# A two-block transformer on one core: memory projections moved behind layer a, rotations by norm-scaled tables on VectorE, layer b's staging and rotation buffers parted

## The chip, the cores and the metric

The kernel runs on one core of a Trainium2 chip. A time is the device time of one execution in microseconds (us), and the number that counts is the median over the runs shown: 2902.65 us for the kernel before (three runs, 2900.12 to 2906.84). All data are float32; matrix products are done in three passes on a 32-bit matmul type (fp32r).

## The reference, cut to what matters

Two transformer blocks run in a row on 512 tokens of width 2048. The first one puts 16 meta tokens ahead (528 columns), then layer a (differential attention) and layer b (windowed attention with sinks); the second one mixes three token mixers and ends in a cross attention to 256 memory tokens.

```python
# layer a
h = rms_norm(x, norm_g)
q, k, v, gate = jnp.split(h @ w_in, 4, axis=-1)        # 8 heads; q, k in two halves of 128 rows
q = partial_rope(q, cos, sin); k = partial_rope(k, cos, sin)   # 32 of the 128 rows are rotated
o = diff_attention(q, k, v, lam, cid)
x = x + (rms_norm(o, subln_g) * (1 - lambda_init) * jax.nn.silu(gate)) @ w_out
# shared k, v of layer b, then layer b
k, v = jnp.split(rms_norm(x, kv_norm) @ w_kv, 2, axis=-1); k = partial_rope(k, cos, sin)
q, gate = jnp.split(rms_norm(x, norm_g) @ w_in, 2, axis=-1); q = partial_rope(q, cos, sin)
x = x + (swa_sink_attention(q, k, v, sinks) * jax.nn.silu(gate)) @ w_out
# second block, at its end: the memory's k and v need nothing but mem
k, v = jnp.split(rmsnorm(mem, norm_mem) @ w_kv_2, 2, axis=-1)
```

## The kernel before, in words

Activations are kept transposed: a tile has 128 features on its partitions and 528 tokens (two halves of 264) along its rows. A product `a @ w` in full accuracy is made of three matmuls: both operands are split into a high part (ScalarE copies to fp32r: `wh` of a weight, `OPH` of an activation) and a low part (VectorE subtracts: `wl`, `OPL`), and `mm3` adds high x high, low x high and high x low in PSUM. `K.proj` (L396) does one tile of 128 output features over 16 blocks of 128 inputs; `ev` then takes the sum out of PSUM (tile `pj`, three buffers). Weights come from HBM on SyncE's queue in chunks in the order of `plan` (L59); `w_next` (L381) keeps the split three pieces ahead of the matmuls.

The norm of a layer's input is a factor per token, so it is applied after the product: `norm_events` (L532) forms the factor from the sums of squares and spreads it over 128 partitions into `rbc`.

Attention is background work: a queue of generators, `K.bg`, of which `K.tick` (called once for each `mm3`) makes a step whenever `K.rate` has added up to one; `K.at` starts something at a given tick. The framework's scheduler then orders each engine's instructions by a timing of its own, so the program's order is not quite that of the code.

Four stages matter here. *Startup* (L568): the first three gate tiles of layer a (`FIRST`) are computed while x is still being loaded, block by block: each of 16 blocks needs x split, its squares added up (`add_sq`, ScalarE squares, GpSimd adds: L529) and one weight piece split. In the same stretch `mem_prep` (L596) splits the memory and adds up its squares, and the memory's k and v are projected right behind. *Layer a* (L674): per head the gate, v, q and k tiles; `rope` (L708) rotates 32 rows of each q and k tile with one shuffle on VectorE and three operations on GpSimd (tables `trig`). *out_a* (L890): the output projection, x added, sums of squares. *Layer b* (L918): k and v, then four units of q tiles and of gate tiles (`q0`, `g0`, ...); `rope` (L936) is the same on 128 rows. `windows` (L967) reads k and v back from HBM in window order. In layer b the tiles `sh` (of `rope`), `ext` (what is written to HBM), `ke` and `vx` (what is read back) share one buffer, tag `"sh"`.

Of the kernel before, what the change touches and what calls it, by code (L numbers as in the profile page):

```python
# [20 lines left out]
P = 128  # L21
# [37 lines left out]
def plan():  # L59
# [18 lines left out]
    for m in range(4):  # L78
        fm("xkv", r(128) + 128 * m)
    tm("xkv", r(512) + 512, 2)  # L80
# [183 lines left out]
class Core:  # L264
# [87 lines left out]
    def w_dma(self, i):  # L352
        while self.wi_dma <= min(i, len(self.chunks) - 1):
            off, kc, n = self.chunks[self.wi_dma]
            t = self.rp.tile([P, 1056], F32, tag="wraw", name="wraw", bufs=3)
            self.nc.sync.dma_start(
                t[:, 0:kc * n], self.a["w"][off:off + P * kc * n].rearrange("(p e) -> p e", p=P))
            self.raw[self.wi_dma] = t
            self.wi_dma += 1
# [208 lines left out]
def startup(K, dbg):  # L568
    nc, tc, a = K.nc, K.tc, K.a
    with ExitStack() as c:  # L570
        sp = c.enter_context(tc.tile_pool(name="sp", bufs=1))
        psp = c.enter_context(tc.tile_pool(name="ps_s", bufs=2, space=PSUM))
        memH = sp.tile([P, KT, NMEM], R, name="memH")
        memL = sp.tile([P, KT, NMEM], R, name="memL")
        msq = sp.tile([P, NMEM], F32, name="msq")
        rm = sp.tile([P, 5], F32, name="rm")
        rmb = sp.tile([P, NMEM], F32, name="rmb")
        xr, mr = {}, {}

        def load_x(k):  # L580
            if k < KT:
                xr[k] = sp.tile([P, T], F32, tag="xr", name="xr", bufs=4)
# [8 lines left out]
        def load_mem(i):  # L591
            if i < 4:
                mr[i] = sp.tile([P, 4, NMEM], F32, tag="mr", name="mr", bufs=2)
                nc.sync.dma_start(mr[i], a["mem"][:, 4 * i:4 * i + 4, :])

        def mem_prep():  # L596
            load_mem(0)
            load_mem(1)
            for k in range(KT):
                t = mr[k // 4][:, k % 4]  # L600
                K.split(memH[:, k], memL[:, k], t, scale=K.vcol("norm_mem_2", k))
                if k == 0:
                    nc.vector.tensor_tensor(msq, t, t, ALU.mult)
                else:
                    sq = sp.tile([P, NMEM], F32, tag="msqk", name="msqk", bufs=2)
                    nc.vector.tensor_tensor(sq, t, t, ALU.mult)
                    nc.gpsimd.tensor_tensor(msq, msq, sq, ALU.add)
                if k % 4 == 3:
                    load_mem(k // 4 + 2)
                yield  # L610


        load_x(0)
        nc.sync.dma_start(K.vec, a["vec"])
# [3 lines left out]
        K.w_dma(1)  # L618
        make_identity(nc, K.ident)
# [5 lines left out]
        K.rate = 18 / 42  # L625
        K.bg.append(mem_prep())
# [22 lines left out]

        def first_gates():  # L650
            for (h, s), f in zip(FIRST, fs):
                nc.vector.tensor_tensor(f, f, K.rbc, ALU.mult)
                th = sp.tile([P, T], F32, tag="th", name="th")
                K.act(th, f, AF.Tanh, scale=0.5)
                nc.vector.scalar_tensor_tensor(K.H[:, 2 * h + s], th, 1.0, f, ALU.add, ALU.mult)
                yield
        K.at(t0 + 12, lambda: K.bg.append(first_gates()))
        norm_events(K, sp, psp, "n", 1e-6, 0, NMEM, (t0 + 8, t0 + 15), rm, rmb, acc=msq)
        for m in range(4):
            def ev(ps, c0, c1):  # L660
                o = sp.tile([P, NMEM], F32, tag="xo", name="xo", bufs=2)
                nc.vector.tensor_tensor(o, ps, rmb, ALU.mult)
                nc.sync.dma_start(K.xkvd[:, m * NMEM:(m + 1) * NMEM], o)
            K.proj(ev, ((0, NMEM),), memH, memL)

        def evv(ps, ti, ci):
            o = sp.tile([P, 512], F32, tag="xov", name="xov", bufs=2)
            nc.scalar.activation(o, ps, AF.Copy, scale=rm[:, ti:ti + 1])
            nc.sync.dma_start(K.xkvd[:, 1024 + ti * 512:1024 + (ti + 1) * 512], o)
        K.proj_tm(evv, ((0, P), (P, 2 * P)), 512, [K.psj], memH, memL)  # L670
        K.drain()


def layer_a(K, dbg):  # L674
    nc, tc, a = K.nc, K.tc, K.a
    with ExitStack() as c:
# [20 lines left out]
        K.at(t0 + 4, lam)  # L697
# [10 lines left out]
        def rope(f):  # L708
# [140 lines left out]
        for h, base in ORDER_A:  # L849
# [5 lines left out]
            for s in range(2):  # L855
# [3 lines left out]
                K.proj(ev_scaled(f), HALVES)  # L859
# [30 lines left out]
def out_a(K, dbg):  # L890
    nc, tc, a = K.nc, K.tc, K.a
    with ExitStack() as c:
        op = c.enter_context(tc.tile_pool(name="oap", bufs=1))
        for k in range(KT):
            K.split(K.OPH[:, k], K.OPL[:, k], K.H[:, k])
        xr = {}
# [6 lines left out]
        load(1)  # L903
        for m in range(KT):
            load(m + 2)
            x = xr.pop(m)

# [4 lines left out]
            K.add_sq(op, K.H[:, m], m == 0)  # L912

# [4 lines left out]
def layer_b(K, dbg):  # L918
    nc, tc, a = K.nc, K.tc, K.a
    with ExitStack() as c:  # L920
# [30 lines left out]

        for m in range(4):
            f = bp.tile([P, T], F32, tag="f", name="f", bufs=2)
            K.proj(ev_scaled(f), HALVES)
            if m < 2:
                rope(f, 0, T)
            e = bp.tile([P, TX], F32, tag="sh", name="ext")
# [5 lines left out]
        kv = {}  # L963
        done = set()
# [982 lines left out]
```

## Time and profile before

| | |
|---|---|
| median of three runs | 2902.65 us (2900.12 to 2906.84) |
| the profiled execution | 2901.79 us, span 2900.1 us |
| TensorE (PE) busy | 2833.7 us, 98% of the span |
| VectorE (DVE), ScalarE (ACT), GpSimd (POOL) busy | 1711.9, 1302.0, 641.3 us |
| mean granted TensorE clock | 0.989 |

The span runs from the first to the last instruction; 1.7 us of the execution lie around it. Matmuls are pipelined: a matmul's own duration is over twice the distance to the next one, so the pace is read from how many start in a stretch. Idle time is given with what ended it, and only where the profile sees the engine wait.

### The profile page before, as it was taken

How to read it: one execution, taken by the hardware profiler on the slowest of the kernel's cores; microseconds unless marked ns; L12 is line 12 of the kernel's file. 1: busy time of each engine (PE TensorE's matmuls, PEld its weight loads, DVE VectorE, ACT ScalarE, POOL GpSimd, SP SyncE). 2: the span in 40 equal slices, each digit the busy share in tenths (PEclk: the TensorE clock that was granted, in tenths of full speed). 3: DMA queues.
4: the chain of work that ended last, by engine and by line, in shares of the span. 5: the costliest groups of instructions: out<-in, count | busy, mean ns of one | idle time of the engine just before them, and what ended most of it. 6: DMA issues, size and time to landing. Idle time of an engine off the chain costs nothing. (4 is left out here: it accounts for less than half of the span.)

```text
span 2900.1 us, 45499 instructions
## 1 busy us (share of the span) xinstructions
PE 2833.7 (98%) x17664; PEld 2534.4 (87%) x17664; DVE 1711.9 (59%) x3307; ACT 1302.0 (45%) x2892; POOL 641.3 (22%) x572
## 2 busy tenths in 40 slices
PE   7999999999999999989999999999999999999997
PEld 7999999999999999878877888888888877788887
DVE  8445555555566435576767733565556488774375
ACT  5333333333335323454656633455555356552253
POOL 5022022022221011123211012122332135131103
PEclk9999999999999999999999999999999999999999
DMA  5422222222222443322222243322222223224332
GB/s 184 156 87 75 74 81 81 73 81 80 74 74 66 137 137 117 123 66 73 70 78 69 73 166 130 106 81 88 77 83 89 88 81 113 82 92 128 105 113 70
DMA packets 92936, 277.05 MB, mean 96 GB/s; under 512 B 10112, under 2 KB 18192, under 8 KB 92720
## 3 DMA queue, kind: packets, MB, share of 16 engines
q1 hardware_dynamic: 91904, 273.37, 29.2%
q8 instruction: 138, 2.26, 0.3%
q10 hardware_dynamic: 816, 0.79, 0.1%
q14 instruction: 78, 0.64, 0.1%
HBM read 257.11 MB, written 17.01 MB: 95 GB/s over the span
## 5 line engine op out<-in xcount | busy, mean ns | idle before, releaser
L258 PE MATMUL pj<-OPH,wh 128*128 128x264 f32 (+1 forms) x4416 | 1459.3, 332 | 7.5 <-ACT wh L375 6.3
L258 PE MATMUL pj<-OPH,wl 128*128 128x264 f32 (+1 forms) x4416 | 1449.0, 329 | 4.2 <-DVE wl L376 4.1
L258 PE MATMUL pj<-OPL,wh 128*128 128x264 f32 (+1 forms) x4416 | 1441.2, 329 | 11.6 <-DVE OPL L472 11.6
L376 DVE TENSOR_TENSOR wl<-wraw,wh 128x512 fp32r<-128x512 f32 (+2 forms) x868 | 665.4, 769 | 638.0 <-ACT wh L375 633.0
L375 ACT ACTIVATE wh<-wraw 128x512 fp32r<-128x512 f32 (+2 forms) x868 | 544.2, 628 | 1013.8 <-PE pj L258 914.6
L258 PEld LDWEIGHTS pj<-OPH,wh 128*128 128x128 f32 x4416 | 833.1, 189 | 87.3 <-ACT wh L375 6.3
L258 PEld LDWEIGHTS pj<-OPL,wh 128*128 128x128 f32 x4416 | 830.5, 189 | 87.8 <-DVE OPL L472 13.1
L258 PEld LDWEIGHTS pj<-OPH,wl 128*128 128x128 f32 x4416 | 834.3, 189 | 74.0 <-DVE wl L376 5.2
L529 POOL TENSOR_TENSOR sumsq<-sumsq,sq 128x512 f32<-128x512 f32 (+2 forms) x101 | 122.4, 1218 | 547.9 <-ACT sq L528 511.9
L711 POOL TENSOR_TENSOR sh<-sh,trig 32x528 f32<-32x528 f32 x32 | 52.2, 1630 | 649.6 <-DVE sh L710 464.3
L258 PE MATMUL pj<-wh,OPH 128*128 128x260 f32 (+1 forms) x384 | 124.6, 325 | 0.0
L258 PE MATMUL pj<-wh,OPL 128*128 128x260 f32 (+1 forms) x384 | 123.6, 322 | 0.0
L258 PE MATMUL pj<-wl,OPH 128*128 128x260 f32 (+1 forms) x384 | 120.8, 321 | 0.0
L939 POOL TENSOR_TENSOR sh<-sh,trigb 128x512 f32<-128x512 f32 (+1 forms) x18 | 27.3, 1517 | 273.3 <-DVE sh L938 155.4
L306 ACT ACTIVATE p<-S,nmx 128x264 f32<-128x264 f32 (+5 forms) x112 | 49.7, 447 | 74.1 <-DVE nmx L758 36.8
L258 PEld LDWEIGHTS pj<-wh,OPH 128*128 128x128 f32 x384 | 72.6, 189 | 6.9 <-issue 1.5
L306 ACT ACTIVATE st<-st 128x512 f32<-128x512 f32 (+3 forms) x136 | 72.5, 550 | 12.8 <-DVE st L1164 11.1
L705 DVE TENSOR_TENSOR f<-pj,rbc 128x264 f32<-128x264 f32 x122 | 52.4, 430 | 43.4 <-PE pj L258 39.5
L258 PEld LDWEIGHTS pj<-wl,OPH 128*128 128x128 f32 x384 | 72.3, 189 | 6.2
L258 PEld LDWEIGHTS pj<-wh,OPL 128*128 128x128 f32 x384 | 72.9, 190 | 5.1
L468 ACT ACTIVATE ph<-T 80x256 fp32r<-80x256 f32 (+3 forms) x128 | 49.4, 391 | 36.4 <-DVE pl L469 18.1
L469 DVE TENSOR_TENSOR pl<-T,ph 80x256 fp32r<-80x256 f32 (+3 forms) x128 | 54.5, 432 | 14.9 <-ACT ph L468 13.9
(428 smaller groups left out, 3581.6 us busy)
## 6 DMA issues: line engine op xcount, KB each, us to landing
wraw<-in_w SPq DMA_DIRECT2D x410, 512.0 KB, 3.5
xr<-in_x SPq DMA_DIRECT2D x32, 264.0 KB, 3.5
wraw<-in_w SPq DMA_DIRECT2D x16, 520.0 KB, 3.4
xr<-hd SPq DMA_DIRECT2D x32, 256.0 KB, 2.8
hd<-H SPq DMA_DIRECT2D x16, 264.0 KB, 2.1
hd<-H SPq DMA_DIRECT2D x16, 256.0 KB, 2.0
wraw<-in_w SPq DMA_DIRECT2D x16, 256.0 KB, 2.7
wraw<-in_w SPq DMA_DIRECT2D x8, 384.0 KB, 4.7
```

The lines of the kernel that those rows point to most:

```text
L258: return self._put(self.nc.tensor.matmul(*args, **kw))
L306: i = self.nc.scalar.activation(out, in_, func, **kw)
L375: nc.scalar.activation(h[:, 0:kc * n], raw, AF.Copy)
L376: nc.vector.tensor_tensor(l[:, 0:kc * n], raw, h[:, 0:kc * n].bitcast(F32), ALU.subtract)
L468: nc.scalar.activation(hi, src, AF.Copy)
L469: eng.tensor_tensor(lo, src, hi.bitcast(F32), ALU.subtract)
L529: (eng or nc.gpsimd).tensor_tensor(acc[:, c0:c1], acc[:, c0:c1], sq[:, c0:c1], ALU.add)
L705: nc.vector.tensor_tensor(dst[:, c0:c1], ps, K.rbc[:, c0:c1], ALU.mult)
L711: nc.gpsimd.tensor_tensor(sh, sh, trig[:, 1], ALU.mult)
L939: nc.gpsimd.tensor_tensor(sh[:, c0:c1], sh[:, c0:c1], trig[:, 1, c0:c1], ALU.mult)
```

## The change

Memory: `plan` puts the `xkv` weights behind `a_out`; splits, sums and projections of the memory move from startup into `out_a`, the splits as background work (rate 17/300 a tick, from the fourth output tile), the projections behind its last tile. Startup keeps only the three gate tiles: their sums go raw to `H`, and norm, tanh and gating follow in layer a as background steps; `add_sq` of x adds on VectorE; `vec` is loaded on ScalarE's queue; the first weight chunk comes in two DMAs, x has six buffers in place of four.

Rotation: the tables are multiplied by `rbc` once (`rotation`), and `ev_rotated` multiplies the PSUM sum by the table and shuffles straight from PSUM; product and sum of the shuffled part are VectorE's, as is the low part of k in layer a. GpSimd has no part in it any more.

Layer b: `ext`, `ke` and `vx` take the two buffers of tag `"p"` (the attention's probabilities); `sh` is the rotation's alone. `windows` yields four times, not once, ahead of its transposes; the rate is 1/5 until the first attention, and .52 in place of .46 for the last unit.

```diff
@@ plan, w_dma
-    for m in range(4):
-        fm("xkv", r(128) + 128 * m)
-    tm("xkv", r(512) + 512, 2)
...
     for m in range(16):
         fm("a_out", r(128) + 128 * m)
+    for m in range(4):
+        fm("xkv", r(128) + 128 * m)
+    tm("xkv", r(512) + 512, 2)
...
+            cuts = (0, kc * n) if self.wi_dma else (0, kc * n // 2, kc * n)
@@ startup
         def x_prep(k):
-            load_x(k + 3)
+            load_x(k + 4)
...
-            K.add_sq(sp, t, k == 0)
+            K.add_sq(sp, t, k == 0, eng=nc.vector)
...
-        K.bg.append(mem_prep())
...
+                    nc.scalar.activation(K.H[:, 2 * h + s, c0:c1], psf[2 * t + i][:, 0:c1 - c0], AF.Copy)
@@ layer_a
+        def rotation():
+            nc.vector.tensor_tensor(trs, trs, K.rbc[0:32], ALU.mult)
+            nc.vector.tensor_tensor(rot[0:32], rot[0:32], K.rbc[0:32], ALU.mult)
+            for r in range(32, P, 32):
+                nc.scalar.activation(rot[r:r + 32], K.rbc[r:r + 32], AF.Copy)
...
-            nc.vector.stream_shuffle(sh, f[0:32], swap)
-            nc.gpsimd.tensor_tensor(sh, sh, trig[:, 1], ALU.mult)
-            nc.gpsimd.tensor_tensor(f[0:32], f[0:32], trig[:, 0], ALU.mult)
-            nc.gpsimd.tensor_tensor(f[0:32], f[0:32], sh, ALU.add)
+            def ev(ps, c0, c1):
+                nc.vector.tensor_tensor(dst[:, c0:c1], ps, rot[:, c0:c1], ALU.mult)
+                nc.vector.stream_shuffle(sh[:, c0:c1], ps[0:32], swap)
+                if c1 == T:
+                    nc.vector.tensor_tensor(sh, sh, trs, ALU.mult)
+                    nc.vector.tensor_tensor(dst[0:32], dst[0:32], sh, ALU.add)
...
-                    K.split(hi, lo, f, scale=None if w else SC_A, eng=nc.gpsimd if w else nc.vector)
+                    K.split(hi, lo, f, scale=None if w else SC_A)
@@ out_a
+        K.rate = 17 / 300
...
+            if m == 3:
+                K.bg.append(mem_prep())
@@ layer_b
+            def ev(ps, c0, c1):
+                nc.vector.tensor_tensor(dst[:, c0:c1], ps, trig[:, 0, c0:c1], ALU.mult)
+                nc.vector.stream_shuffle(sh[:, c0:c1], ps, swap)
+                nc.vector.tensor_tensor(sh[:, c0:c1], sh[:, c0:c1], trig[:, 1, c0:c1], ALU.mult)
+                nc.vector.tensor_tensor(dst[:, c0:c1], dst[:, c0:c1], sh[:, c0:c1], ALU.add)
...
-            e = bp.tile([P, TX], F32, tag="sh", name="ext")
+            e = bp.tile([P, TX], F32, tag="p", name="ext", bufs=2)
...
-                ke = bp.tile([P, TX], F32, tag="sh", name="ke")
+                ke = bp.tile([P, TX], F32, tag="p", name="ke", bufs=2)
...
-            vx = bp.tile([P, TX], F32, tag="sh", name="vx")
+            vx = bp.tile([P, TX], F32, tag="p", name="vx", bufs=2)
...
-            yield
+            for _ in range(4):
+                yield
...
-                K.rate = .46
+                K.rate = .46 if u < 3 else .52
```

Where instructions stand now, at two places. VectorE in startup, before, from the first memory work on (`msq`, `msqk` and `memL` are the memory's, `OPL` and `wl` the low parts of x and of the weights):

```order
L603 TENSOR_TENSOR msq<-mr 128x256
L606 TENSOR_TENSOR msqk<-mr 128x256 x2
L472 SCALAR_TENSOR_TENSOR memL<-mr,vec,memH 128x256 x4
L606 TENSOR_TENSOR msqk<-mr 128x256
L376 TENSOR_TENSOR wl<-wraw,wh 128x384
L606 TENSOR_TENSOR msqk<-mr 128x256
L472 SCALAR_TENSOR_TENSOR OPL<-xr,vec,OPH 128x528
L472 SCALAR_TENSOR_TENSOR memL<-mr,vec,memH 128x256 x4
```

The same engine and stretch now:

```order
L474 SCALAR_TENSOR_TENSOR OPL<-xr,vec,OPH 128x528
L378 TENSOR_TENSOR wl<-wraw,wh 128x384
L531 TENSOR_TENSOR sumsq<-sumsq,sq 128x528
L474 SCALAR_TENSOR_TENSOR OPL<-xr,vec,OPH 128x528
L378 TENSOR_TENSOR wl<-wraw,wh 128x384
L531 TENSOR_TENSOR sumsq<-sumsq,sq 128x528
```

The memory's operations are gone from between the two low parts, and the sum of squares, GpSimd's before, stands in their place.

VectorE in layer b before, from the first shuffle of unit q0 to its second query split (`vw` is made from the transposed `vx`, `qp` is the query split; the three products between shuffle and `qp` are GpSimd's and not in this row):

```order
L938 STREAM_SHUFFLE sh<-f 128x512
L469 TENSOR_TENSOR vw<-T,vw 128x2x64 x2
L469 TENSOR_TENSOR vw<-T,vw 80x2x64 x2
L376 TENSOR_TENSOR wl<-wraw,wh 128x512
L938 STREAM_SHUFFLE sh<-f 128x512
L376 TENSOR_TENSOR wl<-wraw,wh 128x512
L469 TENSOR_TENSOR qp<-f,qp 64x8x64 x2
L945 TENSOR_TENSOR f<-pj,rbc 128x512
```

And now, from the same tile on:

```order
L958 TENSOR_TENSOR f<-pj,trigb 128x512
L959 STREAM_SHUFFLE sh<-pj 128x512
L378 TENSOR_TENSOR wl<-wraw,wh 128x512
L960 TENSOR_TENSOR sh<-sh,trigb 128x512
L961 TENSOR_TENSOR f<-f,sh 128x512
L378 TENSOR_TENSOR wl<-wraw,wh 128x512
L471 TENSOR_TENSOR qp<-f,qp 64x8x64 x2
```

Before, the sums of the first two q tiles and most of the `vw` stand ahead of the first shuffle; now it follows its own tile's sum, ahead of the first `vw`, and the whole rotation is in VectorE's row. On TensorE the first score matmul of layer b (`S<-kxh,qp`) stands 48 projection matmuls behind the last of unit q0 before, and 36 now.

## Rows read from the trace of the kernel before

**Rows 1.** The page: busy time, share of the span, instructions.
```profile
PE 2833.7 (98%) x17664; PEld 2534.4 (87%) x17664; DVE 1711.9 (59%) x3307; ACT 1302.0 (45%) x2892; POOL 641.3 (22%) x572
```
**Rows 2.** Busy time of each engine by stage, all engines.
```profile
core 0: us, PE busy (x) PEld busy (x) DVE busy (x) ACT busy (x) POOL busy (x), PEclk, DMA share, GB/s
0.00:61.00 61.00, 42.91 (x288) 41.14 (x289) 54.88 (x70) 37.61 (x71) 39.56 (x36) 0.94 0.56 185
61.00:109.00 48.00, 48.00 (x318) 43.67 (x317) 32.06 (x72) 23.17 (x39) 0.00 (x0) 1.00 0.59 188
109.00:965.00 856.00, 855.29 (x6921) 838.36 (x6919) 474.66 (x1125) 311.30 (x761) 167.37 (x115) 1.00 0.24 79
965.00:1145.00 180.00, 179.80 (x1476) 179.77 (x1477) 68.91 (x116) 58.27 (x95) 19.92 (x15) 1.00 0.42 138
...
1215.00:1260.00 45.00, 36.98 (x164) 29.86 (x163) 30.09 (x52) 16.50 (x43) 19.30 (x12) 0.89 0.21 71
1260.00:1650.00 390.00, 380.01 (x1971) 316.00 (x1970) 276.70 (x606) 233.21 (x684) 72.08 (x48) 0.99 0.22 72
```
**Rows 3.** TensorE's timeline at the start: start, length, then idle time before.
```profile
6.33 1.69 PE L258 MATMUL pj<-OPH,wh 128*128 128x264 f32 x6 [6.33 <-ACT wh L375]
...
12.47 0.28 PE L258 MATMUL pj<-OPH,wl 128*128 128x264 f32 x1
```
**Rows 4.** What TensorE waited for, 0 to 62 us: total, times, longest.
```profile
PE pj L258 <- DVE OPL L472: 11.6, 6, 3.3
```
**Rows 5.** VectorE by line and form, 0 to 60 us: busy, mean ns.
```profile
L472 DVE SCALAR_TENSOR_TENSOR OPL<-xr,vec,OPH 128x528 fp32r<-128x528 f32 x16 | 17.7, 1107 | 1.9 <-ACT OPH L471 1.9
L376 DVE TENSOR_TENSOR wl<-wraw,wh 128x384 fp32r<-128x384 f32 x16 | 17.0, 1074 | 0.7 <-ACT wh L375 0.7
L472 DVE SCALAR_TENSOR_TENSOR memL<-mr,vec,memH 128x256 fp32r<-128x256 f32 x16 | 12.8, 854 | 0.0
L606 DVE TENSOR_TENSOR msqk<-mr 128x256 f32<-128x256 f32 x15 | 8.2, 559 | 0.0
```
**Rows 6.** The same, 61 to 115 us, where GpSimd has no instruction.
```profile
L376 DVE TENSOR_TENSOR wl<-wraw,wh 128x512 fp32r<-128x512 f32 x35 | 24.1, 690 | 15.5 <-ACT wh L375 15.4
...
L652 DVE TENSOR_TENSOR f<-f,rbc 128x528 f32<-128x528 f32 x3 | 1.9, 706 | 0.6 <-ACT rbc L561 0.6
```
**Rows 7.** VectorE's timeline in startup.
```profile
13.52 0.76 DVE L472 SCALAR_TENSOR_TENSOR OPL<-xr,vec,OPH 128x528 fp32r<-128x528 f32 x1
14.20 0.55 DVE L376 TENSOR_TENSOR wl<-wraw,wh 128x384 fp32r<-128x384 f32 x1
...
28.23 1.67 DVE L376 TENSOR_TENSOR wl<-wraw,wh 128x384 fp32r<-128x384 f32 x1
```
**Rows 8.** GpSimd's timeline beside the last of these.
```profile
27.71 1.78 POOL L529 TENSOR_TENSOR sumsq<-sumsq,sq 128x528 f32<-128x528 f32 x1
```
**Rows 9.** What TensorE waited for in layer b, 1215 to 1650 us.
```profile
PE S L258 <- DVE qp L469: 7.5, 1, 7.5
PE O L258 <- DVE H L1067: 6.7, 5, 3.2
PE T L261 <- DVE vw L469: 1.5, 2, 1.3
```
**Rows 10.** VectorE by line and form, 1215 to 1650 us.
```profile
L376 DVE TENSOR_TENSOR wl<-wraw,wh 128x512 fp32r<-128x512 f32 x115 | 93.6, 817 | 49.7 <-ACT wh L375 48.8
...
L945 DVE TENSOR_TENSOR f<-pj,rbc 128x512 f32<-128x512 f32 x28 | 19.2, 688 | 11.2 <-PE pj L258 11.0
...
L938 DVE STREAM_SHUFFLE sh<-f 128x512 f32<-128x512 f32 x16 | 11.7, 734 | 0.1
```
**Rows 11.** GpSimd by line and form, same stretch.
```profile
L940 POOL TENSOR_TENSOR f<-f,trigb 128x512 f32<-128x512 f32 x16 | 26.1, 1631 | 0.0
...
L939 POOL TENSOR_TENSOR sh<-sh,trigb 128x512 f32<-128x512 f32 x16 | 24.4, 1523 | 254.1 <-DVE sh L938 149.6 <-DVE vw L469 60.1 <-DVE nb L1020 23.7
```
**Rows 12.** A later stretch, busy time by engine.
```profile
2400.00:2450.00 50.00, 46.42 (x205) 37.53 (x204) 42.19 (x63) 27.38 (x52) 27.21 (x23) 0.95 0.32 103
```

More of the change, by code (lines that the diff above doesn't have):

```diff
@@ L355, in w_dma @@
             t = self.rp.tile([P, 1056], F32, tag="wraw", name="wraw", bufs=3)
-            self.nc.sync.dma_start(
-                t[:, 0:kc * n], self.a["w"][off:off + P * kc * n].rearrange("(p e) -> p e", p=P))
+            src = self.a["w"][off:off + P * kc * n].rearrange("(p e) -> p e", p=P)
+            cuts = (0, kc * n) if self.wi_dma else (0, kc * n // 2, kc * n)
+            for e0, e1 in zip(cuts, cuts[1:]):
+                self.nc.sync.dma_start(t[:, e0:e1], src[:, e0:e1])
             self.raw[self.wi_dma] = t
@@ L571, in startup @@
         sp = c.enter_context(tc.tile_pool(name="sp", bufs=1))
[L572 to L578, printed above, removed]
+        psp = c.enter_context(tc.tile_pool(name="ps_s", bufs=3, space=PSUM))
+        xr = {}
         def load_x(k):
             if k < KT:
-                xr[k] = sp.tile([P, T], F32, tag="xr", name="xr", bufs=4)
+                xr[k] = sp.tile([P, T], F32, tag="xr", name="xr", bufs=6)
                 nc.sync.dma_start(xr[k], a["x"][:, k, :])
         def x_prep(k):
-            load_x(k + 3)
+            load_x(k + 4)
             t = xr.pop(k)
             K.split(K.OPH[:, k], K.OPL[:, k], t, scale=K.vcol("a_norm", k))
-            K.add_sq(sp, t, k == 0)
[L591 to L609, printed above, removed]
-                yield
+            K.add_sq(sp, t, k == 0, eng=nc.vector)
+        nc.scalar.dma_start(K.vec, a["vec"])
         load_x(0)
-        nc.sync.dma_start(K.vec, a["vec"])
         K.w_dma(0)
@@ L618, in startup @@
         K.w_dma(1)
+        load_x(3)
         make_identity(nc, K.ident)
@@ L624, in startup @@
         x_prep(0)
-        K.rate = 18 / 42
-        K.bg.append(mem_prep())
         for k in range(KT):
@@ L893, in out_a, with load_mem, mem_prep @@
         op = c.enter_context(tc.tile_pool(name="oap", bufs=1))
+        psn = c.enter_context(tc.tile_pool(name="psn", bufs=2, space=PSUM))
         for k in range(KT):
             K.split(K.OPH[:, k], K.OPL[:, k], K.H[:, k])
-        xr = {}
+        xr, mr = {}, {}
+        memH = op.tile([P, KT, NMEM], R, name="memH")
+        memL = op.tile([P, KT, NMEM], R, name="memL")
+        msq = op.tile([P, NMEM], F32, name="msq")
+        rm = op.tile([P, 5], F32, name="rm")
+        rmb = op.tile([P, NMEM], F32, name="rmb")
+        def load_mem(i):
+            if i < 4:
+                mr[i] = op.tile([P, 4, NMEM], F32, tag="mr", name="mr", bufs=2)
+                nc.sync.dma_start(mr[i], a["mem"][:, 4 * i:4 * i + 4, :])
+        def mem_prep():
+            load_mem(0)
+            load_mem(1)
+            yield
+            for k in range(KT):
+                t = mr[k // 4][:, k % 4]
+                K.split(memH[:, k], memL[:, k], t, scale=K.vcol("norm_mem_2", k))
+                K.add_sq(op, t, k == 0, 0, NMEM, acc=msq, eng=nc.vector)
+                if k % 4 == 3:
+                    load_mem(k // 4 + 2)
+                yield
         def load(m):
@@ L912, in out_a, with evv @@
             K.add_sq(op, K.H[:, m], m == 0)
+        for m in range(4):
+            def ev(ps, c0, c1):
+                o = op.tile([P, NMEM], F32, tag="xo", name="xo", bufs=2)
+                nc.vector.tensor_tensor(o, ps, rmb, ALU.mult)
+                nc.sync.dma_start(K.xkvd[:, m * NMEM:(m + 1) * NMEM], o)
+            K.proj(ev, ((0, NMEM),), memH, memL)
+        def evv(ps, ti, ci):
+            o = op.tile([P, 512], F32, tag="xov", name="xov", bufs=2)
+            nc.scalar.activation(o, ps, AF.Copy, scale=rm[:, ti:ti + 1])
+            nc.sync.dma_start(K.xkvd[:, 1024 + ti * 512:1024 + (ti + 1) * 512], o)
+        K.proj_tm(evv, ((0, P), (P, 2 * P)), 512, [K.psj], memH, memL)
 RT = ((NM, T),)
@@ L963, in layer_b @@
         kv = {}
+        K.rate = 1 / 5
         done = set()
```

82 lines of the change are left out of this document (35 added, 47 removed).

## The prediction

> **What bounds the kernel now.** I read the page first, then busy time by stage, then TensorE's waits, and only then the timelines where it waits. TensorE is busy 98% of the span [rows 1] and the change takes no matmul away, so only two things can be won: time in which TensorE stands, and time in which it runs slowly. The view by stage [rows 2] says where: layer a loses 0.7 us of 856, out_a 0.2 of 180, the memory's projections nothing of 48. Startup loses 18.1 of 61, layer b 8.0 of the first 45 and 10.0 of the next 390. All the rest of the kernel is untouched, in work and in order, and I give it no term.
>
> In startup TensorE starts at 6.33 us [rows 3] and has done its 288 matmuls by 61, which is 54.7 us. In out_a, where nothing is waited for, 1476 matmuls, nearly all of the same size, take 179.8 us, 0.1218 us each [rows 2]; at that pace 288 are 35.1 us. So 19.6 us are lost after the first matmul: the 29 matmuls up to 12.47 take 6.1 us where 3.5 would do (start to start twice as far as later), 2.6 us; six waits for the low part of x are 11.6 us [rows 4]; the other 5.4 fit a granted clock of 0.94 [rows 2], which is 12% of 61 us at 1.2 GHz, or 3.7 us lost, and small gaps.
>
> Why is the low part late? VectorE is busy 54.9 of 61 us [rows 2]. Its two operations for a block of x take 1107 and 1074 ns in the mean [rows 5], but 0.76 and 0.55 us where GpSimd is idle, and the 0.55 becomes 1.67 while a GpSimd addition runs [rows 7, 8]: VectorE's subtraction began at 28.23 and ended at 29.90, 0.4 us after GpSimd's addition (27.71 to 29.49). So GpSimd holds VectorE up. It does this in layer b too: the weight split is 817 ns in the mean there and 690 where GpSimd has nothing to do [rows 10, 6].
>
> **Startup.** The memory's work goes from VectorE: 16 x 0.854 + 15 x 0.559 = 22.1 us [rows 5]. GpSimd's additions go; those of x come to VectorE, 15 operations of 128x528. The nearest row is a product of that size, 0.706 us [rows 6]. VectorE then has 16 x (0.76 + 0.55) + 15 x 0.706 = 31.6 us of work, 2.0 a block, against 18 x 0.1218 = 2.19 us of TensorE. That is tight, but it leaves TensorE as the bound. ScalarE (37.6 us of 61 with the memory's copies [rows 2]) and the DMA (185 GB/s in that stretch; x and weights without the memory, 16 x 0.27 + 8 x 0.39 MB, are 7.4 MB, 40 us at that rate, and they begin 4 us ahead of the first matmul) lie below. The six waits and the slow spells behind them go; the slow first 29 matmuls stay, and I leave 1.5 us of gaps. Gain 19.6 - 2.6 - 1.5 = 15.5 us, and 0.4 us from an earlier first matmul (half a chunk lands sooner, and `vec` isn't ahead of it; between 0 and 0.9). Upper bound 17.9; the lower one is rival 1's, 9.
>
> **What follows startup.** The raw gate sums, their norm and the gates (three products of 0.706 us, as before, and two more for the tables) move into layer a, where VectorE is busy 475 of 856 us. The tables' DMAs stand on SyncE's queue among layer a's first weights and need room that x held; three chunks are in front. I take 0; a chunk that is late would cost at most what a block's wait cost here, 3.3 us [rows 4].
>
> **Layer a.** VectorE gets two products of up to 0.706 us (32 rows of 528) for each of 32 tiles, a second shuffle, about 0.1 more, and 16 low parts of k: 32 x 1.5 + 16 x 0.706 = 60 us, less what GpSimd's products cost it. Its share goes from 55% to at most 62%, and TensorE waits for 0.7 us in all. Term 0, bounds -0.7 and +4. A sum is held in PSUM through one more operation of some 0.4 us; the third buffer covers that.
>
> One rule speaks against this. The rows show no surcharge for reading PSUM: the sum's product, 128x512 from PSUM, takes 688 ns, the weight split of that size from SBUF 690 [rows 10, 6]. The Trainium skill ("VectorE: DVE Perf Modes", section "The TRN2 errata — SBUF-src ops pay a fixed extra latency per instruction") gives 120 cycles as the fixed part from PSUM and 58 from SBUF; an estimate by that page is 65 ns for each of the 84 shuffles that now read PSUM (two for each of 32 and 2 tiles, one for each of 16), 5 us of VectorE's time over the kernel, which would be hidden. The measurement decides.
>
> **The memory in out_a.** 48 us of matmuls stand behind the last output tile in place of 61 us; they ran at full pace before while VectorE was busy 32.1 of 48 us. In out_a VectorE is at 68.9 of 180 us [rows 2], so 16 x (0.854 + 0.559) = 22.6 us more, at the held-up price of startup [rows 5], finds room. The splits end before the last tile, and the norm before the first projection. Term 0; bounds 0 and +4 (one late weight chunk, as above).
>
> **Layer b.** The largest wait is the first score matmul's, 7.5 us for the query splits [rows 9]. Before, the first rotation can't write `sh` until `vx`, in the same buffer, has been transposed; four tiles of three GpSimd products of 1.52 to 1.63 us [rows 11] then come late. Now a tile's rotation is 0.69 + 0.73 + 0.69 + 0.69 = 2.8 us of VectorE, and with the two query splits (each a ScalarE copy and a VectorE subtraction, taken at the weight split's 0.69 us) the last tile is ready some 5.5 us after its last matmul. The score stands 36 matmuls of 512 columns behind it, 0.1218 x 512 / 264 = 0.236 us each, 8.5 us, so the wait goes, and with it most of the slow spell: clock 0.89 over 45 us is 9.9 us at 1.2 GHz, of which 7.5 are the wait and the other 2.4 cost 1.2 us. The five waits of the values for VectorE's addition, 6.7 us, come from a VectorE that is 71% busy and held up. It gets 16 x 2 x 0.69 = 22.1 us more and loses 115 x 0.127 = 14.6 us on the weight split alone; its share stays near 72%, without the stalls. I take half of those waits, 3.4, and 1 us of slow clock behind them (0.99 over 390 us is 7.8 us at the low level, at most 3.9 lost); 1 us from the small ones. The wait for `vx` (1.5) I leave: `vx` now shares its buffers with the probabilities, and GpSimd's gates stay. Gain 7.5 + 1.2 + 3.4 + 1 + 1 = 14.1 us. Upper bound: all 18 us and 2.5 of clock, 20.5. Lower bound: 8.7, less as much again for the values as now, 2.0.
>
> **Sum.** 15.9 + 14.1 = 30.0 us. The profiled execution took 2901.8 us, 0.9 under the median of the runs shown; 2901.8 - 30.0 = 2871.8, so **2872 us**.
>
> **Rivals.** *1. VectorE is slow by itself, not held up.* Then 1.107 and 1.074 us stay: 16 x 2.18 + 15 x 0.706 = 45.5 us of VectorE from some 5 us on, startup ends near 51 in place of 45, a gain of 9; in layer b only the first wait goes (8.7) and 22 us more of VectorE's work cost some 4. 2901.8 - 9 - 8.7 + 4 = 2888. Rows 7 and 8 speak against it. *2. Layer b gives only its first wait:* four operations of the rotation now stand together in front of the value additions, which are as late as before. 2901.8 - 15.9 - 8.7 = 2877, and up to 2884 if those waits double. For it speaks that VectorE stays above 70%. *3. Slower: VectorE becomes the bound in layer a.* From 2400 to 2450 us it is busy 84% and TensorE stands 3.6 of 50 us [rows 12]. If the rotations brought layer a there, 7.2% of 856 us are 61 us: 2872 + 61 = 2933. The point is a share near 84%; the rows make it 62%, and a stretch's share can exceed the mean. The Trainium skill ("Perfetto Trace Analysis", section "Optimizing Scalar/DVE Operations") lets work of a saturated VectorE go to other engines, the opposite of this change, but warns that GpSimd shares a read port with it; the trace agrees with the warning. *4. The change does nothing for startup* because x or weights land late: then 2901.8 - 14.1 = 2888. DMA is at 0.56 of its time there.
>
> **How the numbers follow.** Forecast 0.78 (2864 to 2881 by itself), rival 2 0.09, rivals 1 and 4 0.08, rival 3 0.05. The low end, 2863, is both upper bounds (17.9 + 20.5); the high end, 2885, takes in rival 2 and leaves 1, 3 and 4 out. No change means within 0.2% (5.8 us), about what runs of this kernel can tell apart: only a part of rival 3 could end there, 0.01, or above, 0.04.
>
> **What would show it.** Startup: first projection of layer a (`pj` for v) near 45 us, `OPL` and the 128x384 `wl` near 0.76 and 0.55 us, no wait for `OPL` over 1 us. Layer b: no wait of `S` for `qp` above 1 us, `wl` at 0.70 to 0.75 us. GpSimd's busy time falls from 641 to some 350 us. Layer a and the memory's stretch behind out_a keep TensorE busy to within 2 us. If startup's projections end after 50 us, or a new wait for `wl` or `f` shows in layer a, the prediction is wrong there.

## The result, and the profile after

The changed kernel takes 2872.93 us (median of four runs, 2871.73 to 2874.63), the kernel before 2903.01 (2900.12 to 2906.84): a ratio of 0.9896, 95% interval 0.9879 to 0.9913. The forecast was 2872. Beside the last experiment it ran again: 2872.15 us, ratio 0.9891 (0.9874 to 0.9907).

From the page after, busy time, share and instructions, against [rows 1]: GpSimd gives up 283 us, VectorE's total stays.

```profile
PE 2829.0 (98%) x17664; PEld 2531.1 (88%) x17664; DVE 1709.3 (59%) x3513; ACT 1305.9 (45%) x2911; POOL 358.1 (12%) x376
```

Busy time by stage after, the counterparts of [rows 2]: startup, layer a, out_a, the memory's projections, and two stretches of layer b.

```profile
core 0: us, PE busy (x) PEld busy (x) DVE busy (x) ACT busy (x) POOL busy (x), PEclk, DMA share, GB/s
0.00:45.00 45.00, 39.30 (x310) 39.30 (x311) 32.58 (x62) 31.17 (x56) 0.70 (x6) 1.00 0.67 219
45.00:917.00 872.00, 871.46 (x7049) 854.16 (x7048) 493.67 (x1302) 322.28 (x783) 5.29 (x4) 1.00 0.25 81
917.00:1097.00 180.00, 180.00 (x1487) 179.81 (x1486) 89.91 (x151) 68.90 (x123) 18.71 (x14) 1.00 0.45 146
1097.00:1145.00 48.00, 48.00 (x308) 43.63 (x307) 25.38 (x65) 17.62 (x29) 0.00 (x0) 1.00 0.55 171
1187.00:1232.00 45.00, 45.00 (x213) 36.77 (x212) 27.89 (x61) 19.18 (x54) 0.00 (x0) 1.00 0.28 94
1232.00:1622.00 390.00, 379.92 (x1982) 316.35 (x1981) 276.78 (x636) 234.87 (x687) 20.56 (x14) 1.00 0.23 73
```

The stages were measured from the start of a stage's first matmul into `pj` to that of the next stage's; the last one ends with the start of the last matmul, and some 11 us behind it are in no column. The memory's stage stands behind startup before, and behind out_a after. In us, of the profiled executions:

| kernel | first matmul | startup's 288 | layer a | out_a | memory | kv | layer b | out_b | rest |
|---|---|---|---|---|---|---|---|---|---|
| before | 6.33 | 54.75 | 838.0 | 189.1 | 48.2 | 49.3 | 472.7 | 178.5 | 1052.1 |
| after | 5.70 | 36.71 | 840.5 | 190.0 | 46.4 | 48.2 | 460.8 | 178.6 | 1054.9 |
| after, again | 5.68 | 36.48 | 840.5 | 189.8 | 46.4 | 48.2 | 462.3 | 178.6 | 1050.9 |

So the spans, 2900.1 and 2872.9 us, differ by 0.6 + 18.0 for startup, 11.9 for layer b, less 0.5 for the four stages between and out_b, less 2.7 in the rest, which the change doesn't touch. That 2.7 isn't a loss: the same kernel gives 1050.9 in the second profile, and the twelve profiles of this document that leave the rest as it was give 1049.3 to 1054.9. In the same way the changed startup takes 36.5 to 37.8 us in the nine profiles that have it, and the changed layer b 460.1 to 462.5 in eight. A difference within these bounds says nothing.

What TensorE waited for after, 0 to 1625 us (total, times, longest); compare [rows 4, 9].

```profile
PE O L258 <- DVE H L1089: 6.2, 7, 1.7
PE pj L258 <- ACT wh L377: 5.7, 1, 5.7
PE S L258 <- ACT kxh L473: 2.4, 1, 2.4
PE pj L258 <- DVE sh L959: 1.4, 1, 1.4
...
```

The 5.7 is the wait until the first matmul. All waits for `OPL` are gone, and so are those of `S` for `qp` and of `T` for `vw`. The values' wait for the addition, `O <- H`, is nearly what it was (6.7 in five); those for `kxh` and `sh` are new.

TensorE's timeline at the start (start, length, idle time before), against [rows 3]: the slow spacing of 0.22 us lasts to 9.34 us, not to 12.47, and none of it is a wait.

```profile
5.70 1.69 PE L258 MATMUL pj<-OPH,wh 128*128 128x264 f32 x6 [5.70 <-ACT wh L377]
7.19 0.42 PE L258 MATMUL pj<-OPH,wl 128*128 128x264 f32 x1
...
9.34 0.28 PE L258 MATMUL pj<-OPH,wl 128*128 128x264 f32 x1
```

VectorE by line and form, 0 to 43 us (busy, mean ns of one), against [rows 5]:

```profile
L474 DVE SCALAR_TENSOR_TENSOR OPL<-xr,vec,OPH 128x528 fp32r<-128x528 f32 x16 | 11.9, 766 | 2.3 <-ACT OPH L473 2.3
L531 DVE TENSOR_TENSOR sumsq<-sumsq,sq 128x528 f32<-128x528 f32 x15 | 10.6, 706 | 0.2
L378 DVE TENSOR_TENSOR wl<-wraw,wh 128x384 fp32r<-128x384 f32 x16 | 8.6, 555 | 0.1
```

The three prices, 0.77, 0.71 and 0.56 us, are, within 0.01 us, those that the forecast used. The same view of layer b, 1187 to 1622 us, against [rows 10]:

```profile
L378 DVE TENSOR_TENSOR wl<-wraw,wh 128x512 fp32r<-128x512 f32 x118 | 85.3, 723 | 52.9 <-ACT wh L377 51.8
L1089 DVE TENSOR_TENSOR H<-sumsq,O 64x256 f32<-64x256 f32 x64 | 26.7, 417 | 9.7 <-ACT sumsq L1088 8.7
...
L1056 DVE TENSOR_SCALAR p<-p,sums 128x208 f32<-128x208 f32 x48 | 14.8, 344 | 0.4
...
L959 DVE STREAM_SHUFFLE sh<-pj 128x512 f32<-128x512 f32 x15 | 11.0, 735 | 0.0
```

### The profile page after: what moved, and what is told of

The parts are those of the page before. It is cut to its first block, busy times and chain, and to the rows that moved or that the text cites. A ratio compares the mean times of both kernels' runs of the same rounds, so it can differ in the third digit from the quotient of the medians.

```text
span 2872.9 us, 45386 instructions
## 1 busy us (share of the span) xinstructions
PE 2829.0 (98%) x17664; PEld 2531.1 (88%) x17664; DVE 1709.3 (59%) x3513; ACT 1305.9 (45%) x2911; POOL 358.1 (12%) x376
## 5 line engine op out<-in xcount | busy, mean ns | idle before, releaser
L378 DVE TENSOR_TENSOR wl<-wraw,wh 128x512 fp32r<-128x512 f32 (+2 forms) x868 | 629.4, 727 | 629.3 <-ACT wh L377 623.4
L531 POOL TENSOR_TENSOR sumsq<-sumsq,sq 128x512 f32<-128x512 f32 (+2 forms) x86 | 98.3, 1150 | 555.1 <-ACT sq L530 519.4
L1139 POOL TENSOR_TENSOR H<-H,th 128x512 f32<-128x512 f32 x14 | 21.0, 1513 | 524.1 <-DVE H L1089 475.8
L306 ACT ACTIVATE st<-st 128x512 f32<-128x512 f32 (+3 forms) x136 | 72.5, 550 | 14.1 <-DVE st L1185 12.5
L471 DVE TENSOR_TENSOR pl<-T,ph 80x256 fp32r<-80x256 f32 (+3 forms) x128 | 54.5, 432 | 10.9 <-ACT ph L470 9.9
L261 PE MATMUL T<-ident,p 128*128 128x128 f32 (+3 forms) x392 | 59.9, 271 | 0.8 <-DVE p L1826 0.7
```

The source lines that it names most:

```text
L261: return self._put(self.nc.tensor.transpose(*args, **kw))
L306: i = self.nc.scalar.activation(out, in_, func, **kw)
L378: nc.vector.tensor_tensor(l[:, 0:kc * n], raw, h[:, 0:kc * n].bitcast(F32), ALU.subtract)
L471: eng.tensor_tensor(lo, src, hi.bitcast(F32), ALU.subtract)
L531: (eng or nc.gpsimd).tensor_tensor(acc[:, c0:c1], acc[:, c0:c1], sq[:, c0:c1], ALU.add)
L1139: e.tensor_tensor(dst, dst, th, ALU.mult)
```

## The experiments

Theory: GpSimd's operations lengthen VectorE's, in startup and in layer b, and the change wins by taking them away. Rivals: VectorE simply had too much work; the parted buffers do it; the order of the loads does it. Unless a ratio is given, a total is one run, beside a run of the kernel before on the same chip (2903.03 us for the first four, 2903.88 for the next four, 2902.92 for the two after them).

**Startup: x's squares added on GpSimd again.**

```
-            K.add_sq(sp, t, k == 0, eng=nc.vector)
+            K.add_sq(sp, t, k == 0)
```

> The changed kernel, with the fifteen additions of the squares of x in startup put back on GpSimd and nothing else. Theory (GpSimd's additions hold VectorE up): the low part of x and the 128x384 weight split rise from 0.77 and 0.55 us to about 1.1 and 1.07 us in the mean, 2.2 us of VectorE a block against 2.19 us of TensorE, so the 288 matmuls of startup take 37 to 40 us in place of 36.7; most of startup's gain stays. Rival (VectorE was only overloaded by the memory's operations): both durations stay at 0.77 and 0.55 us and startup stays at 36.7 us.

Measured: 2880.91 us, startup's matmuls 45.26 us, 8.5 us more than after and well past the 37 to 40 that the theory gave. VectorE, and GpSimd's additions, 0 to 45 us:

```profile
L474 DVE SCALAR_TENSOR_TENSOR OPL<-xr,vec,OPH 128x528 fp32r<-128x528 f32 x16 | 21.9, 1396 | 1.6 <-ACT OPH L473 1.6
L378 DVE TENSOR_TENSOR wl<-wraw,wh 128x384 fp32r<-128x384 f32 x16 | 14.1, 901 | 2.6 <-ACT wh L377 2.6
```

```profile
L531 POOL TENSOR_TENSOR sumsq<-sumsq,sq 128x528 f32<-128x528 f32 x15 | 24.0, 1603 | 12.1 <-ACT sq L530 11.1
```

The two operations that TensorE waits for take 36.0 us in place of 20.5 (11.9 + 8.6 above). Fifteen additions on GpSimd thus cost VectorE 15.5 us, 1.03 each; on VectorE itself they cost 10.6, 0.71 each. That is the theory's mechanism, and more of it than was expected: 2.30 us of VectorE a block against 2.19 of TensorE, so TensorE waits for the weight split and for `OPL`:

```profile
...
PE pj L258 <- DVE wl L378: 5.2, 3, 3.3
PE pj L258 <- DVE OPL L474: 0.7, 1, 0.7
```

The granted clock then is 0.96 in the first 45 us, 1.00 after the change.

**Startup: the memory's preparation as well, on VectorE alone.** It is `mem_prep` of the kernel before with its additions on VectorE, drained behind startup's last matmul; its output is read by nobody, the projections use the one made in out_a.

```
+                    nc.vector.tensor_tensor(sq, t, t, ALU.mult)
+                    nc.vector.tensor_tensor(msq, msq, sq, ALU.add)
...
+        K.rate = 18 / 42
+        K.bg.append(mem_prep())
...
```

> The changed kernel with the memory's loads, splits and squares done in startup as well, a copy that nobody reads, all of it on VectorE and none on GpSimd. Theory (hold-up and work both count): without GpSimd an operation of the memory of 128x256 costs about 0.42 us, three of them 1.26 us a block, so VectorE needs 0.77 + 0.55 + 0.71 + 1.26 = 3.3 us a block and the 288 matmuls take some 50 to 53 us in place of 36.7, while the low part of x stays at 0.77 us. Rival (only GpSimd's sharing mattered): startup stays within 2 us of 36.7.

Measured: 2875.75 us, startup 37.29 us. The theory's 50 to 53 was wrong, the rival right. VectorE by form, 0 to 62 us:

```profile
L474 DVE SCALAR_TENSOR_TENSOR OPL<-xr,vec,OPH 128x528 fp32r<-128x528 f32 x16 | 12.1, 766 | 1.4 <-ACT OPH L473 1.4
...
L474 DVE SCALAR_TENSOR_TENSOR memL<-mr,vec,memH 128x256 fp32r<-128x256 f32 x16 | 6.8, 484 | 0.0
L610 DVE TENSOR_TENSOR msq<-msq,msqk 128x256 f32<-128x256 f32 x15 | 6.3, 423 | 0.1
L609 DVE TENSOR_TENSOR msqk<-mr 128x256 f32<-128x256 f32 x15 | 6.2, 422 | 0.0
```

The memory's operations are 19.3 us here; they fill the gaps, and what finds none runs after startup (12 of the 16 `memL` by 45 us). TensorE waits for none of them, and 37.29 us lies within what startup takes without them (36.5 to 37.8). So VectorE had room for this work in startup all along, as long as GpSimd stood still. It isn't shown that the memory's projections could have stayed right behind startup: the last of its sums ends at 57.7 us, some 15 us after startup's matmuls, and no run put the projections there.

**Startup: the memory's preparation, with both kinds of additions on GpSimd.** As above (again read by nobody), with

```
-                    nc.vector.tensor_tensor(msq, msq, sq, ALU.add)
+                    nc.gpsimd.tensor_tensor(msq, msq, sq, ALU.add)
-            K.add_sq(sp, t, k == 0, eng=nc.vector)
+            K.add_sq(sp, t, k == 0)
```

> The changed kernel with the memory's loads, splits and squares done in startup as well, a copy that nobody reads, with the additions of x's and the memory's squares on GpSimd as before the change. Theory: startup is back at its length before, 53 to 56 us for the 288 matmuls, with the low part of x near 1.1 us and waits for it of some 11 us, since these operations alone were the cause. Rival (the tokens, buffers or the order of the loads that the change also altered gave part of the gain): startup stays under 51 us.

Measured: 2892.93 us, startup 53.43 us, as the theory gave; the waits add up to the 11 us expected, but 4.9 of them are for `wl` and 5.8 for `OPL`. This run and the one before it do the same work, and only the engine of the additions differs: that alone is 16.1 us. The `memL` that took 484 ns without GpSimd takes 821 here:

```profile
L474 DVE SCALAR_TENSOR_TENSOR OPL<-xr,vec,OPH 128x528 fp32r<-128x528 f32 x16 | 19.2, 1207 | 2.1 <-ACT OPH L473 2.1
L378 DVE TENSOR_TENSOR wl<-wraw,wh 128x384 fp32r<-128x384 f32 x16 | 14.8, 933 | 0.0
L474 DVE SCALAR_TENSOR_TENSOR memL<-mr,vec,memH 128x256 fp32r<-128x256 f32 x16 | 12.3, 821 | 0.0
```

Taken in this order, startup's 16.7 us (53.4 to 36.7) fall into 8.5 for x's additions and 8.2 for the memory with its additions. What else the change does in startup (loads, buffers) is worth at most the remaining 1.3 (54.75 to 53.43), which is no more than startup varies by.

**Layer a: rotations and the low parts of k on GpSimd again.**

```
...
-                    nc.vector.tensor_tensor(sh, sh, trs, ALU.mult)
-                    nc.vector.tensor_tensor(dst[0:32], dst[0:32], sh, ALU.add)
...
+                    nc.gpsimd.tensor_tensor(sh, sh, trs, ALU.mult)
+                    nc.gpsimd.tensor_tensor(dst[0:32], dst[0:32], rot[0:32], ALU.mult)
+                    nc.gpsimd.tensor_tensor(dst[0:32], dst[0:32], sh, ALU.add)
...
```

> The changed kernel with layer a's rotations, and the low parts of k, on GpSimd again, on tables that are not scaled by the norm. Theory (layer a is bound by TensorE and hides either): layer a's projections take 840 us within 1.5 us, and TensorE waits for VectorE less than 2 us there; the weight splits on VectorE get longer in the mean, at no cost. Rival (VectorE's rotations cost the 2.5 us by which layer a got longer): layer a is 2 us shorter, 838 us.

Measured: 2873.63 us, layer a 840.7 us. Where these rotations run decides nothing. Of the 2.5 us by which layer a got longer, 2.3 are the 20 matmuls of x's norm (by the trace, start to start), which stood in the memory's stage before; that one got 1.8 shorter.

**Layer b: rotations on GpSimd, buffers parted.**

```
...
-                nc.vector.tensor_tensor(sh[:, c0:c1], sh[:, c0:c1], trig[:, 1, c0:c1], ALU.mult)
-                nc.vector.tensor_tensor(dst[:, c0:c1], dst[:, c0:c1], sh[:, c0:c1], ALU.add)
...
+                nc.gpsimd.tensor_tensor(dst[:, c0:c1], dst[:, c0:c1], trig[:, 0, c0:c1], ALU.mult)
+                nc.gpsimd.tensor_tensor(sh[:, c0:c1], sh[:, c0:c1], trig[:, 1, c0:c1], ALU.mult)
+                nc.gpsimd.tensor_tensor(dst[:, c0:c1], dst[:, c0:c1], sh[:, c0:c1], ALU.add)
...
```

> The changed kernel with layer b's rotations on GpSimd again (three products each, on tables that are not scaled by the norm), while the staging buffers stay parted. Theory (the first wait came from the shared buffer, the rest from GpSimd holding VectorE): the first wait of the scores for the query splits stays away, since no rotation waits for vx, but the weight split goes back to about 0.80 us in the mean; layer b's projections take 463 to 467 us in place of 461, and 473 before. Rival (the rotations' engine set the first wait): a wait of S for qp above 4 us is back and layer b takes 468 us or more.

Measured: 2876.88 us, layer b 467.3 us, 0.3 above the theory's range. The wait for `qp` stays away, as the theory has it; the values' wait grows, and the weight split is back at 814 ns. TensorE's waits in layer b, then VectorE by form:

```profile
PE O L258 <- DVE H L1089: 11.5, 8, 2.4
PE pj L258 <- DVE f L958: 0.8, 1, 0.8
PE S L258 <- ACT p L306: 0.5, 1, 0.5
```

```profile
L378 DVE TENSOR_TENSOR wl<-wraw,wh 128x512 fp32r<-128x512 f32 x118 | 95.9, 814 | 50.2 <-ACT wh L377 49.3
L1089 DVE TENSOR_TENSOR H<-sumsq,O 64x256 f32<-64x256 f32 x62 | 25.8, 416 | 8.9 <-ACT sumsq L1088 7.8
...
L1056 DVE TENSOR_SCALAR p<-p,sums 128x208 f32<-128x208 f32 x48 | 19.5, 443 | 0.5
```

The trace says how the one leads to the other. Of the values' 11.5 us, four waits of 8.2 us together are for an addition that stands behind a scaling of `p` or a query split which ran beside GpSimd and took 1.0 to 1.7 us; without GpSimd these take 0.32 and 0.69. Ahead of the longest wait, 2.4 us, it is two scalings (GpSimd's products run from 1464.34 to 1468.76):

```profile
1464.74 2.28 DVE L1056 TENSOR_SCALAR p<-p,sums 128x208 f32<-128x208 f32 x2
```

**Layer b: rotations on VectorE, one staging buffer.**

```
-            e = bp.tile([P, TX], F32, tag="p", name="ext", bufs=2)
+            e = bp.tile([P, TX], F32, tag="sh", name="ext")
```

and the same for `ke` and `vx`.

> The changed kernel with the extended keys and values and their windows staged in the one buffer of the rotations again, while the rotations stay on VectorE. Theory (a rotation of 2.8 us on VectorE catches up after vx has been transposed): the first wait of S for qp is below 2 us, and layer b takes 461 to 464 us. Rival (parting the buffers is what removed the wait): that wait is 4 us or more, and layer b takes 466 us or more.

Measured: 2875.03 us, layer b 462.0 us, inside what the changed layer b itself takes (460.1 to 462.5). TensorE's waits there:

```profile
PE O L258 <- DVE H L1089: 5.1, 6, 1.6
PE pj L258 <- DVE sh L959: 2.3, 2, 1.4
PE T L261 <- DVE vw L471: 2.0, 1, 2.0
```

No wait for `qp` at all, though the buffer is still waited for. VectorE's first shuffle of unit q0, before and here, is released by a transpose (`T`) of `vx`:

```profile
1227.71 0.01 DVE L938 LOAD_MASK_SELECT sh<-f  x1 [0.19 <-PE T L261]
```

```profile
1206.35 0.01 DVE L959 LOAD_MASK_SELECT sh<-pj  x1 [0.62 <-PE T L261]
```

Counted from q0's first matmul, that is 42.0 us before and 37.4 here; in the changed kernel it is 13.3. Four rotations then end with the last query split at 68.1 us before, 10.7 behind the start of the first score, and at 56.9 here, 2.5 ahead of it: on VectorE they catch up. Both runs keep the new rate and the four `yield`s of `windows`, but these aren't what decides: the transposes of `vx` start 22.3 to 22.8 us after q0's first matmul in all four kernels.

Either edit alone thus removes the first wait. With the rotations on VectorE, parting the buffers is worth nothing measurable; with the buffers parted, the new engine is worth some 5 us (467.3 against 460.1 to 462.5).

**Layer b alone.** The kernel before, with the changed layer b.

> The kernel before with layer b alone replaced by the changed one. Theory (the two halves of the gain are independent): layer b takes 460 to 463 us, all else is as before, and the whole takes 2903 - 11 = 2892 us, within 3. Rival (layer b gains through what the rest of the change leaves in front of it): layer b stays above 466 us and the whole above 2896 us.

Measured: 2889.57 us, 14.3 less than the kernel before beside it; layer b 462.5 us, which is 10.2 of them; startup (54.5) and the rest (1050.2) are as they were, within what they vary by. Layer b's gain doesn't need the other half of the change.

**The values' wait: two halves of a bank.**

```
...
-                        if x[1] == 0:
-                            po[x[0]] = psO.tile([P, 512], F32, tag="O", name="O")
-                        values(x[0], x[1], po[x[0]])
+                        values(x[0], x[1], o_bank)
```

`o_bank` is one tile of 512 columns, made once for the layer.

> The changed kernel with layer b's value sums written into the halves of one PSUM bank that is held for the whole layer, so that the products of one half wait for the addition of that same half only, and not for both halves of the window before. Theory (the values wait because the buffer comes free one half too late): the seven waits of O for the addition on VectorE, 6.2 us, fall below 2.5 us and layer b takes 456 to 459 us. Rival (VectorE is late with every addition by more than the spacing of the halves): the waits stay above 4 us and layer b at 460 to 462 us.

Measured: 2874.55 us, layer b 459.7 us, and the wait unchanged to the digit, 6.2 us in seven, the longest 1.7. The theory was wrong on what is waited for. In the changed kernel's own trace five of the seven waits are of a window's second half for the addition of the same window's first half, and two are of a first half for the addition of the second half before it. One of the five (first TensorE, then VectorE):

```profile
1288.96 0.36 PE L258 MATMUL O<-ph,vw 128*128 128x256 f32 x1
...
1292.55 0.38 PE L258 MATMUL O<-ph,vw 128*128 128x256 f32 x1 [1.04 <-DVE H L1089]
```

```profile
1290.10 0.66 DVE L378 TENSOR_TENSOR wl<-wraw,wh 128x512 fp32r<-128x512 f32 x1
1290.68 0.41 DVE L471 TENSOR_TENSOR pl<-T,ph 128x256 fp32r<-128x256 f32 x1
1291.02 0.68 DVE L960 TENSOR_TENSOR sh<-sh,trigb 128x512 f32<-128x512 f32 x1
1291.61 0.56 DVE L1056 TENSOR_SCALAR p<-p,sums 128x208 f32<-128x208 f32 x2
1292.09 0.41 DVE L1089 TENSOR_TENSOR H<-sumsq,O 64x256 f32<-64x256 f32 x1
```

In this program's order the unit that is held is the bank, not the half; and the addition, whose copy on ScalarE was done at 1290.45, stood behind four rows of other work, a rotation's product among them. Of all seven waits, four (3.2 us) stand behind a rotation's product or sum, two (2.5 us) behind query splits, and one (0.6 us) behind a weight split. The Trainium skill ("PSUM — Partial Sum Buffer", section "Terms") says that TensorE writing a bank while VectorE or ScalarE reads it in the same partitions is an error; the order seen here keeps them apart by the bank too.

**The values' wait: both parts copied out by ScalarE.**

```
+                nc.scalar.activation(hd, o[r].rearrange("p (j q) -> p j q", j=4), AF.Copy)
+                nc.vector.tensor_tensor(hd, hd, vo[r], ALU.add)
```

in place of VectorE's addition from PSUM; `hd` is the same slice of `K.H`.

> The changed kernel with both parts of a value sum of layer b copied out of PSUM by ScalarE, and VectorE's addition done on the copies. Theory (the sum's one PSUM bank comes free late because the addition that reads it stands behind the rotation's operations in VectorE's queue): the waits of O for the addition, 6.2 us in seven, fall below 2 us, and layer b takes 455 to 459 us in place of 460.8 to 462.5; ScalarE has 64 copies of 0.38 us, 24 us, more to do. Rival (ScalarE's queue takes VectorE's place as what is late): the waits stay above 4 us, now for ScalarE's copy, and layer b stays at 461 us or above.

Measured: 2861.69 us, layer b 452.2 us, below the theory's range. TensorE's waits in layer b:

```profile
PE O L258 <- ACT H L1090: 1.1, 2, 0.7
PE T L261 <- ACT p L1054: 0.8, 2, 0.6
PE O L258 <- DVE pl L471: 0.6, 2, 0.4
PE S L258 <- ACT kxh L473: 0.2, 1, 0.2
```

So the addition's lateness was the cause: once the bank no longer waits for it, the values' waits are 1.7 us, and those for `kxh` and `sh` shrink too (2.4 to 0.2 and 1.4 to none; why isn't shown).

**Behind layer b: five of GpSimd's products on VectorE.** One of five like edits (L1207, L1454, L1466, L1504, L1540):

```
-                    nc.gpsimd.tensor_tensor(ev[:, :, f], ev[:, :, f], kv[:, :, f], ALU.mult)
+                    nc.vector.tensor_tensor(ev[:, :, f], ev[:, :, f], kv[:, :, f], ALU.mult)
```

> The changed kernel with five of GpSimd's products of the gated linear attention and of the head norms behind layer b moved to VectorE (26.8 us of GpSimd's time between 2260 and 2530 us, some 11 us of VectorE's). Theory (an operation on GpSimd costs VectorE more than the operation itself: in startup fifteen additions of 1.6 us made VectorE's two operations of a block longer by 0.98 us, against 0.71 us for the addition on VectorE): the weight split falls from 0.84 to 0.78 us or less in that stretch and the part from 1807 us on gets 3 to 7 us shorter than its 1050 to 1055 us. Rival (VectorE, 75% busy there, becomes the bound): that part is as long or longer, with more waits for the weight split.

Measured: 2865.25 us; the rest takes 1045.7 us. The weight split, 2260 to 2530 us, in the changed kernel and here:

```profile
L378 DVE TENSOR_TENSOR wl<-wraw,wh 128x512 fp32r<-128x512 f32 x71 | 59.5, 842 | 26.9 <-ACT wh L377 24.2 <-PE pj L258 2.1 <-PE lv L258 0.4
```

```profile
L378 DVE TENSOR_TENSOR wl<-wraw,wh 128x512 fp32r<-128x512 f32 x73 | 54.1, 745 | 23.4 <-ACT wh L377 20.9 <-PE pj L258 2.1 <-PE lv L258 0.4
```

VectorE's total there rises from 201.6 to 207.1 us only, and the rest is 3.6 us shorter than in the best of the twelve profiles that leave it alone. So five products on GpSimd cost more than on VectorE outside the change too. How the gain comes about isn't settled: the wait for `wl` (3.1 us, now 3.4) stays, and a moved product is also done sooner itself (L1504 takes 1007 ns on GpSimd, 511 on VectorE), so that what hangs on it comes earlier; TensorE's waits for `lkl` go from 2.0 to 0.8 us in that stretch. No run parts this from the hold-up.

**Both together, and the changed kernel again.**

> The changed kernel once more, beside the kernel before and the next one on the same chip, to compare with that next one. All theories: 2871 to 2875 us, a ratio of 0.989 to 0.991 to the kernel before.

> The two last edits together: layer b's value sums copied out of PSUM by ScalarE, and the five products of the gated linear attention and the head norms on VectorE. Theory (they act in different stretches and add up): layer b's projections take 452 to 455 us, the part from the end of out_b on 1043 to 1048 us, and the whole 2852 to 2858 us, a ratio near 0.983 to the kernel before. Rival (the gains of single profiles, 11 and 8 us, are partly differences of the clock between executions): 2859 to 2866 us.

Measured: 2855.93 us (2854.43 to 2857.40), ratio 0.9838 to the kernel before (0.9823 to 0.9852), against 2872.15 us and 0.9891 (0.9874 to 0.9907) for the changed kernel beside it. Layer b takes 452.6 us, the rest 1042.5: both gains stand in one kernel, as the theory has it. It is faster than the changed kernel and than the one before.

## Why the prediction came out right

The time was met within 1 us, but by luck: two errors cancel. Startup gained 2.8 us more than its term, layer b 2.2 less.

*Startup, 15.9 us; measured 18.7 (18.0 + 0.6 for the first matmul).* The mechanism held: no wait for `OPL`, 0.77 and 0.56 us, TensorE the bound. The term mis-sized is what was left standing, 2.6 us for the slow first matmuls and 1.5 for gaps. 36.71 us against 35.1 at out_a's pace leaves 1.6 for both, and 16 slow matmuls at 0.1 us too much each are all of it: there are no gaps. The slow stretch itself differs between executions of the same startup, 13 to 26 matmuls in the nine profiles, which is why startup takes 36.5 to 37.8 us; its granted clock reads 1.00, and what slows it stays open. By these profiles the term is 17.6 to 18.9 us, so a part of the 2.8 is this execution's. The working was wrong in one more place, which the sum doesn't show: it took the memory's 22.1 us off VectorE as if that were a term. It wasn't the work that cost, which adds nothing measurable on VectorE, but GpSimd's additions.

*Between, 0; measured 0.5 lost over four stages and out_b.* The term held. VectorE's share of layer a is 57%, below the 62 given as the most; rival 3's 84% was far off. The tables' DMAs made no weight late. No surcharge shows for reading PSUM: the shuffle takes 735 ns from PSUM, 734 from SBUF before [rows 10]. The Trainium skill ("VectorE: DVE Perf Modes", section "The TRN2 errata — SBUF-src ops pay a fixed extra latency per instruction") would have it 65 ns longer, an estimate by that page; the measurement decides.

*Layer b, 14.1 us; measured 11.9, and 10.2 to 12.6 over the eight profiles.* The first wait went, the granted clock of that stretch rose from 0.89 to 1.00, and `vx` did even better than forecast, its 1.5 gone. The step that failed is "I take half of those waits, 3.4": it took a less crowded VectorE to be an earlier one. The values' waits went from 6.7 to 6.2: the addition now queues behind the rotations' own operations in four of the seven (3.2 us), and behind query and weight splits in the other three, of which one, 0.8 us, is there before as well. Two new waits (2.4 and 1.4) came. That is rival 2's mechanism in part. Where ScalarE frees the bank in the addition's place, layer b gets another 8 to 10 us shorter (452.2 against 460.1 to 462.5).

*Rival 1* fell by the first experiment: VectorE's operations are slow only beside GpSimd. *Rival 4* fell with startup. Also, "the first rotation can't write `sh` until `vx` has been transposed" was true, but parting the buffers wasn't needed: with one buffer the shuffle still stands until `vx` is transposed, and the rotations on VectorE make up for it.

## What to carry to other kernels

Price an elementwise operation on GpSimd by what it adds to VectorE's operations beside it (here 1.03 us for each addition of 1.6), not as free; where that is more than VectorE would take itself, move it. Ask not how busy an engine is but which of its operations the bound engine waits for: 19 us more on VectorE cost nothing measurable in startup, while an addition of 0.41 us that came late cost 6.2 in seven waits. And when a change takes two causes of one wait away, test each alone; one of them may be doing nothing.

## What the hardware showed that was not expected

GpSimd slows only some of VectorE's operations. With GpSimd's rotations in layer b the weight split goes from 723 to 814 ns and the scaling of `p` from 344 to 443, but the addition from SBUF and PSUM stays at 417 and 416, as the product of the sum from PSUM did before (688 in the mean with GpSimd's rotations [rows 10], 685 after). These means mix operations that met GpSimd with others that didn't; parted by the trace of the kernel before, 99 weight splits of layer b that met none took 688 ns in the mean, and 28 that ran at least 30% of their time beside a GpSimd operation 1214. The scaling of `p` takes 321 and 939 ns in the same way, but the addition 418 (52 of them) and 411 (11). The Trainium skill ("SBUF — State Buffer", section "Who interferes with whom") says so: an operation with two inputs from SBUF, or a scaling in its two-port mode, shares a port with GpSimd, one with at most one SBUF input outside that mode does not. The traces agree in both directions; whether the scaling ran in that mode no row shows.
